# Two of six modulation tiles of a pair: scaled on ScalarE, added to the running sum by an accumulating transfer

## The chip, the cores and the metric

The kernel runs on one core of a Trainium2 chip. The metric is the device time of one execution in microseconds, and the number that counts is the median of the runs shown. The core has five engines that run side by side, each with an in-order queue of its own: TensorE (PE; its weight loads are listed apart as PEld), VectorE (DVE), ScalarE (ACT), GpSimd (POOL) and SyncE (SP, which here only issues transfers). Transfers run on 16 DMA engines, whoever issues them.

## The reference, cut to what matters

A two-layer trunk: layer 0 is RWKV-7 time mixing and a squared-ReLU MLP, layer 1 chunked band attention and a second MLP, with D = 2048 and 256 time steps. Every sub-layer is shifted, scaled and gated by a modulation vector that comes from one conditioning vector c:

```python
mod = c @ w_ada[layer] + b_ada[layer]              # (1, 2048) @ (2048, 12288)
sh1, sc1, gt1, sh2, sc2, gt2 = jnp.split(mod, 6, axis=-1)
h = modulate(rms_norm(x, g_mix[layer]), sh1, sc1)
y = rwkv7_time_mix(h, ...)                         # heads of 64; r, k, v, decay, a, g; a scan over time
x = x + gt1[:, None, :] * y
```

The modulation is a product of one vector with a large matrix, so almost all of its cost is in bringing the matrix in and passing over it once. Nothing of layer 0 after the time mixing, and nothing of layer 1, can start without its parts.

## The kernel before, in words

All matrix products run in split precision: a weight tile of 128x1024 is loaded (`raw`), ACT casts it to the high half `wH`, DVE subtracts to get the low half `wL` (`halves`, lines 413 to 424), and PE multiplies with both (`proj`, `proj2`).

The time mixing is the loop over slots of lines 1062 to 1100. The 2048 channels are 16 pairs of heads (128 channels each). A pair takes 8 slots of dense work on PE (its k and r products: `proj_steps`), and each pair also goes through 36 small steps, one to a slot: 8 early (decay, key norm, the scaled operands), 12 that invert a triangular matrix (`tt`, `u`, `iv`, with the masks `al` made by POOL), and 16 late (the recurrence over four chunks, group norm, gate). The small steps of several pairs share a slot, so each slot has: the small products of the live pairs, then two steps of dense products, then background work. From slot 128 on, the dense work is the output projection (`out_steps`).

The background work of a slot hangs on `(slot + lead) % S`, with S = 8, called the slot's remainder below. At 1, 3, 6 and 7 a weight tile is halved (`w_make`). At 0, 1, 2, 4, 6 and 7, from the second pair on, one modulation tile is stepped (`ada`, `ada_step`). The sum of a modulation half (1024 columns) is made in one buffer, `acc`, which is 128 rows of partial sums: 16 tiles of 128x1024, one for each row block `kt` of the matrix. Tile 0 sets the sum with one tensor_scalar (line 499), tiles 1 to 15 add to it with one scalar_tensor_tensor on DVE (line 501): `acc = raw * c[kt] + acc`. After tile 15, 32 small products on PE (`ada_sum`) add up the rows, and DVE adds the bias (line 527). `ADA_A` = 111 tiles are stepped in this stage; the rest follow in later stages.

A modulation tile is loaded by SP into a ring of three buffers (`rada`, `ada_room(3)`); `ada_fill` issues a load as soon as fewer than two tiles wait. SP also issues the weight loads, in one queue with these.

What sets the order: the program is traced in the order of the loop, and a planner then orders each engine's queue by its own estimates of when operands are there. `issue_after` and `behind` pin some work behind a named instruction of the same engine: the background work stands behind the last marked small step on ACT and on DVE. Nothing is marked on POOL or SP. Semaphores hold an instruction until its operands are there, and everything behind it on that engine waits with it.

POOL's work in this stage is small elementwise steps of the pairs: lines 180, 188, 190, 201, 205 of the early steps, 255, 256, 259 and 284 of the inversion. No transfer is issued by POOL anywhere in the kernel.

Of the kernel before, what the change touches and what calls it, by code (L numbers as in the profile page):

```python
# [14 lines left out]
AF = mybir.ActivationFunctionType  # L15
ALU = mybir.AluOpType
# [5 lines left out]
KT = D // P  # L22
# [347 lines left out]
class Body:  # L370
# [116 lines left out]
            self.ada_q.append((key, half, kt, raw))  # L487
        return tile_ is not None

    def ada_step(self):  # L490
        nc = self.nc
        if not (self.ada_q or self.ada_load()):
            return
        key, half, kt, raw = self.ada_q.popleft()
        ck = self.ct[:, kt:kt + 1]
        if kt == 0:
            self.fin(HK)
            self.acc = self.wp.tile([P, HK * P], F32, tag="acc", bufs=1, name="acc")
            nc.vector.tensor_scalar(out=self.acc, in0=raw, scalar1=ck, scalar2=0.0, op0=ALU.mult, op1=ALU.add)
        else:  # L500
            nc.vector.scalar_tensor_tensor(out=self.acc, in0=raw, scalar=ck, in1=self.acc, op0=ALU.mult, op1=ALU.add)  # L501
        if kt == KT - 1:
            self.fins = self.ada_sum(self.acc, self.mods[key], half, self.ada_src(*key)[1])
            if not self.lazy:
                self.fin(HK)
            if half == KT // HK - 1:
                self.ada_done.add(key)
# [23 lines left out]
        for _ in range(n):  # L531
            next(self.fins, None)

    def ada(self, n=1):
        for _ in range(n):
            self.ada_step()
        self.ada_fill()

    def mark(self, ins):
# [224 lines left out]
    def layer_a(self, st, sp):  # L764
        nc, tc, d = self.nc, self.tc, self.d
# [7 lines left out]
        with ExitStack() as s1:  # L773
# [9 lines left out]
            for q in range(4):  # L783
                (nc.sync if q % 2 else nc.scalar).dma_start(out=h[:, 4 * q:4 * q + 4, 1:T + 1],
                                                            in_=d["x"][:, 4 * q:4 * q + 4, :])
# [197 lines left out]
        with ExitStack() as s1:  # L983
# [16 lines left out]
            def proj_steps(pr):  # L1000
                for dst, hl in (("k", xk), ("r", xr)):
                    if dst == "r" and pr.j < 2:
                        ps = pp.tile([P, 2, T], F32, tag="lt", bufs=2, name="pj")[:, 0, :]
                    else:
                        ps = pp.tile([P, 2 * T], F32, tag="pj", bufs=1, name="pj")[:, :T]
                    for kt in range(KT):
                        if kt % HK == 0:
                            w = [self.w_made.popleft()] * (KT // HK)
                        self.proj(ps, w, lambda kt: hl[:, kt, :, 0:T], (kt, kt + 1))
                        if dst == "k" and kt == 1:  # L1010
                            if pr.j:
                                lw1 = pw.tile([P, 2, P], F32, tag="lw", bufs=1, name="lw")
                                nc.sync.dma_start(out=lw1, in_=d["lora2"][pr.j, :, 0:2])
                            pr.lw = lw1 if pr.j else lw0
                        if kt % 2 == 1:
                            if kt == KT - 1:
                                t = pw.tile([P, T], F32, tag=dst, bufs=2, name=dst)
                                nc.scalar.copy(t, ps)  # L1018
                                setattr(pr, dst, t)
                            yield  # L1020
# [36 lines left out]
            S, lead = self.SLOTS, self.LEAD  # L1057
# [4 lines left out]
            for slot in range(S * NPAIR + Pair.STEPS - lead):  # L1062
                live = []
                for j, pr in enumerate(pairs):
                    at = slot + lead - S * (j + 1)
                    if 0 <= at < Pair.STEPS:
                        if at == 0:
                            pr.gen = pr.steps()
                        sums = at in (Pair.STEPS - 3, Pair.STEPS - 1)
                        live.append((0 if at in inverts else 1 + (at < Pair.EARLY) + 2 * sums, -at, pr))  # L1070
                        pr.done = at == Pair.STEPS - 1
                self.small_steps([(o, -at, pr) for o, at, pr in sorted(live, key=lambda x: x[:2])])
                last = self.last_pe()
                if slot < S * NPAIR:
                    if slot % S == 0:
                        dense = proj_steps(pairs[slot // S])
                    todo = 16 // S
                else:
                    if outs is None:
                        self.y_hl = self.new_hl()  # L1080
                        outs = dense = out_steps()
                    n = int(sum(pace[:slot + 1 - S * NPAIR]))
                    todo, n_out = n - n_out, n
                with tc.issue_after(last):
                    for _ in range(todo):
                        next(dense, None)
                with tc.issue_after(self.last_pe()):
                    self.fin(HK)
                if outs is not None:
                    j = len(self.y_split)  # L1090
                    if j < KT - 1 and pairs[j].done:
                        self.split(self.y_hl, j, v[:, j, :])
                        self.y_split.append(j)
                if slot + lead == 2 * S - 4:
                    self.ada_fill()
                with self.behind():
                    if (slot + lead) % S in (1, 3, 6, 7):
                        self.w_make()
                    if slot + lead >= 2 * S and (slot + lead) % S in (0, 1, 2, 4, 6, 7):
                        self.ada()  # L1100
            for _ in dense:
                pass
            self.ada_drain(3)
# [123 lines left out]
    def attention(self, st, pp, scaled, kv_gain, kv_shift):  # L1227
# [8 lines left out]
        def projected(src, hl, dst, ada, between=()):  # L1236

            between = iter(between)
            w = self.weight(src)
            ps = pp.tile([P, 2, T], F32, tag="pj", bufs=2, name="pj")  # L1240
            for q in range(0, KT, 4):
                ins = self.proj2(ps, w, lambda kt: hl[:, kt, :, 0:T], (q, q + 4))
                with tc.issue_after(ins):
                    next(between, lambda: None)()
            self.sum2(dst, ps)
            self.ada(ada)
# [175 lines left out]
```

## Time and profile before

| | |
|---|---|
| median of 3 runs | 2601.4 us (2600.03 to 2603.03) |
| the profiled execution's own time | 2600.04 us |
| its span, first to last instruction | 2598.3 us |
| DVE accumulates of modulation tiles (line 501), whole kernel | 360, 462.7 us |
| the same that set the sum (line 499), whole kernel | 24 |
| loads of modulation tiles after the first stage | 384 of 512 KB |
| POOL's busy time, whole kernel | 229.2 us, 9% of the span |

How to read it: busy times are unions of an engine's instructions; a matmul's end is modelled, so PE's busy time has some slack in it. In a timeline row the first number is the start in us, the second the length, then engine, line, operation, `out<-in`, shapes and count; a bracket at the end gives how long the engine sat idle before and what released it. In a row of waits stand the total in us, the number of times and the longest. A name like SPq is an engine's queue of issues.

### The profile page before, as it was taken

The page shows a single profiled execution, that of the slowest core. Times are in us where ns is not written, and L with a number is a line of the kernel's source. Part 1 is how long each engine was busy: PE and PEld are TensorE (multiplying, and loading weights), DVE is VectorE, ACT ScalarE, POOL GpSimd, SP SyncE. Part 2 cuts the span into 40 slices and gives each one's busy share as a digit, 9 for nine tenths or more (in the row PEclk, how much of TensorE's full clock was granted, in tenths as well). Part 3 has the DMA queues.
Part 4 walks back from the last instruction along what each step waited for, and adds up shares of the span by engine and source line. Part 5 has one row for each costly group of instructions (what it writes and reads, how often), then busy time and mean ns, then how long its engine had stood idle before and what let it go on. Part 6 is the DMA issues. An engine that isn't in the chain of part 4 may idle for free.

```text
span 2598.3 us, 58875 instructions
## 1 busy us (share of the span) xinstructions
PE 2541.2 (98%) x24018; PEld 2225.7 (86%) x24018; DVE 2075.9 (80%) x3020; ACT 1371.4 (53%) x2535; POOL 229.2 (9%) x336
## 2 busy tenths in 40 slices
PE   6998999999999999999999999999999999999998
PEld 4788888888998888888888988887998888888887
DVE  6888889998899888888889898899896555556555
ACT  3346666674565364464455554565564463553554
POOL 0003333331200000000001000000100000000001
PEclk9999999999999999999999999999999999999999
DMA  9966666667869899888898688887676555555553
GB/s 364 366 232 195 216 213 223 212 217 222 307 220 338 322 329 343 326 323 316 313 323 291 201 305 304 309 277 261 233 258 212 187 187 188 187 188 191 187 187 130
DMA packets 207119, 662.65 MB, mean 255 GB/s; under 512 B 21248, under 2 KB 53632, under 8 KB 206848
## 3 DMA queue, kind: packets, MB, share of 16 engines
q1 hardware_dynamic: 205072, 657.02, 73.1%
q8 instruction: 188, 3.08, 0.5%
q10 hardware_dynamic: 1776, 1.87, 0.2%
q14 instruction: 83, 0.68, 0.1%
HBM read 656.71 MB, written 2.10 MB: 254 GB/s over the span
## 4 chain that ended last, share of the span: by engine, by line
PE 80%; DVE 10%; issue 4%; ACT 3%; DMA 2%; POOL 1%; SPq 0%; ACTq 0%; DVEq 0%; POOLq 0%
PE pj L454 43%; PE pj L456 21%; DVE acc L501 3%; PE pj L443 3%; PE pj L444 2%; PE pj L445 2%; DVE wL L423 2%; PE lt L588 1%; PE o L443 1%; DMA rada<-w_ada 1%; ACT wH L420 1%; PE o L444 1%; PE o L445 1%; ACT da L252 1%; PE pT L1310 0%
## 5 line engine op out<-in xcount | busy, mean ns | idle before, releaser
L423 DVE TENSOR_TENSOR wL<-raw,wH 128x1024 fp32r<-128x1024 f32 x771 | 946.6, 1229 | 336.7 <-ACT wH L420 334.1
L420 ACT CAST wH<-raw 128x1024 fp32r<-128x1024 f32 x771 | 805.3, 1045 | 729.6 <-PE pj L454 579.0
L454 PE MATMUL pj<-aHL,wH 128*128 128x512 f32 x2816 | 894.0, 398 | 1.2 <-DVE x L1135 1.1
L454 PE MATMUL pj<-hHL,wH 128*128 128x512 f32 x2048 | 644.2, 396 | 0.0
L456 PEld LDWEIGHTS pj<-aHL,wL 128*128 128x128 f32 x2816 | 531.7, 189 | 124.2 <-issue 0.3
L456 PE MATMUL pj<-aHL,wL 128*128 128x256 f32 x2816 | 563.0, 281 | 0.0
L501 DVE SCALAR_TENSOR_TENSOR acc<-rada,ct,acc 128x1024 f32<-128x1024 f32 x360 | 462.7, 1285 | 9.5 <-DMA rada<-w_ada 9.1
L456 PEld LDWEIGHTS pj<-hHL,wL 128*128 128x128 f32 x2048 | 384.2, 188 | 91.1 <-DVE wL L423 0.7
L454 PEld LDWEIGHTS pj<-aHL,wH 128*128 128x128 f32 x2816 | 431.6, 189 | 8.9 <-issue 8.5
L456 PE MATMUL pj<-hHL,wL 128*128 128x256 f32 x2048 | 402.0, 278 | 0.3 <-DVE wL L423 0.3
L454 PEld LDWEIGHTS pj<-hHL,wH 128*128 128x128 f32 x2048 | 312.0, 189 | 1.3 <-DVE hHL L1181 1.1
L443 PE MATMUL pj<-aHL,wH 128*128 128x256 f32 (+1 forms) x896 | 263.4, 294 | 1.5 <-ACT r L1018 1.4
L444 PE MATMUL pj<-aHL,wH 128*128 128x256 f32 (+1 forms) x896 | 253.7, 283 | 0.0
L445 PE MATMUL pj<-aHL,wL 128*128 128x256 f32 (+1 forms) x896 | 252.5, 282 | 0.0
L620 POOL TENSOR_TENSOR ss<-ss,sq 128x256 f32<-128x256 f32 x56 | 52.7, 942 | 1579.7 <-ACT sq L619 1532.1
L443 PEld LDWEIGHTS pj<-aHL,wH 128*128 128x128 f32 x896 | 169.8, 189 | 6.1 <-ACT r L1018 2.1
L1206 DVE SCALAR_TENSOR_TENSOR x<-pj,mod,x 128x256 f32<-128x256 f32 x256 | 123.4, 482 | 64.1 <-PE pj L456 61.1
L444 PEld LDWEIGHTS pj<-aHL,wH 128*128 128x128 f32 x896 | 169.6, 189 | 0.8
L445 PEld LDWEIGHTS pj<-aHL,wL 128*128 128x128 f32 x896 | 170.1, 190 | 0.2
L1178 ACT ACTIVATE t<-t 128x256 f32<-128x256 f32 x112 | 46.8, 418 | 119.6 <-DVE t L1150 119.6
L1181 DVE TENSOR_TENSOR hHL<-t,hHL 128x256 fp32r<-128x256 f32 x128 | 53.9, 421 | 1.8 <-ACT t L1180 1.1
L1180 ACT ACTIVATE t<-t 128x256 f32<-128x256 f32 x128 | 53.3, 416 | 3.3
(270 smaller groups left out, 2757.9 us busy)
## 6 DMA issues: line engine op xcount, KB each, us to landing
rada<-w_ada SPq DMA_DIRECT2D x320, 512.0 KB, 5.2
raw<-w_up SPq DMA_DIRECT2D x256, 512.0 KB, 4.1
raw<-w_down SPq DMA_DIRECT2D x256, 512.0 KB, 3.8
rada<-w_ada_kv SPq DMA_DIRECT2D x64, 512.0 KB, 6.3
rawa<-w_ada SPq DMA_DIRECT2D x32, 512.0 KB, 9.1
rawa<-w_ada_t SPq DMA_DIRECT2D x32, 512.0 KB, 8.6
raw<-w_k SPq DMA_DIRECT2D x32, 512.0 KB, 5.0
raw<-w_r SPq DMA_DIRECT2D x32, 512.0 KB, 4.0
```

The costliest lines, as they stand in the source:

```text
L420: nc.scalar.copy(Hf, raw)
L423: eng.tensor_tensor(out=Lf, in0=raw, in1=Hf, op=ALU.subtract)
L443: nc.tensor.matmul(ps, H[:, i, :], a(kt)[:, 0, :], start=(first and kt == 0), stop=False)
L444: nc.tensor.matmul(ps, H[:, i, :], a(kt)[:, 1, :], start=False, stop=False)
L445: ins = nc.tensor.matmul(ps, L[:, i, :], a(kt)[:, 0, :], start=False, stop=(last and kt == KT - 1))
L454: nc.tensor.matmul(ps, w[kt // HK][0][:, kt % HK, :], a(kt), start=(kt == 0), stop=False)
L456: ins = nc.tensor.matmul(ps[:, 0, :], w[kt // HK][1][:, kt % HK, :], a(kt)[:, 0, :], start=False, stop=(kt == KT - 1))
L501: nc.vector.scalar_tensor_tensor(out=self.acc, in0=raw, scalar=ck, in1=self.acc, op0=ALU.mult, op1=ALU.add)
L620: (eng or nc.gpsimd).tensor_tensor(out=self.ss, in0=self.ss, in1=sq, op=ALU.add)
L1180: nc.scalar.activation(t, t, AF.Square)
L1181: nc.vector.tensor_tensor(out=h[:, 1, :], in0=t, in1=h[:, 0, :], op=ALU.subtract)
L1206: nc.vector.scalar_tensor_tensor(out=x, in0=ps[:, i, :], scalar=self.mods[(layer, 5)][:, n:n + 1], in1=x, op0=ALU.mult, op1=ALU.add)
```

## The change

In the slots of remainder 2 and 4 the loop now calls `ada(moved=True)`. A tile that is stepped there, unless it is the first or the last of its sum, is multiplied by c[kt] on ACT in place, and POOL issues a transfer from the tile to `acc` that adds to what is there. The other tiles are stepped as before. An accumulate on DVE that follows a transfer waits for its landing, and so does a transfer that follows another; a tile's buffer can be loaded again once its transfer has landed.

```diff
-    def ada_step(self):
+    def ada_step(self, moved=False):
         ...
+        elif moved and kt < KT - 1:
+            nc.scalar.activation(raw, raw, AF.Copy, scale=ck)
+            nc.gpsimd.dma_start(out=self.acc, in_=raw, accum_op=ALU.add)
         else:
             nc.vector.scalar_tensor_tensor(out=self.acc, in0=raw, scalar=ck, in1=self.acc, op0=ALU.mult, op1=ALU.add)
...
-    def ada(self, n=1):
+    def ada(self, n=1, moved=False):
         for _ in range(n):
-            self.ada_step()
+            self.ada_step(moved)
         self.ada_fill()
...
                     if slot + lead >= 2 * S and (slot + lead) % S in (0, 1, 2, 4, 6, 7):
-                        self.ada()
+                        self.ada(moved=(slot + lead) % S in (2, 4))
```

## The prediction

> **What bounds the kernel now.** I read the page first. PE is busy nearly throughout, but that is a share over stages with different limits, so it says little about this one.
>
> ```profile
> span 2598.3 us, 58875 instructions
> ...
> PE 2541.2 (98%) x24018; PEld 2225.7 (86%) x24018; DVE 2075.9 (80%) x3020; ACT 1371.4 (53%) x2535; POOL 229.2 (9%) x336
> ...
> q1 hardware_dynamic: 205072, 657.02, 73.1%
> ```
>
> The change acts only in time mixing. The windows below (columns: length; busy us and instructions of PE, PEld, DVE, ACT, POOL; granted clock; DMA share; GB/s) cut it out, from the first tile that can be moved to the point where the output projection fills the stage.
>
> ```profile
> 226.00:293.00 67.00, 62.80 (x1502) 56.43 (x1497) 61.51 (x104) 39.81 (x108) 24.98 (x29) 1.00 0.71 226
> 293.00:420.00 127.00, 123.77 (x2971) 111.94 (x2971) 114.89 (x205) 83.23 (x245) 47.13 (x60) 1.00 0.67 215
> 420.00:549.00 129.00, 125.44 (x3039) 113.50 (x3039) 117.60 (x212) 83.76 (x246) 48.96 (x60) 1.00 0.68 221
> 549.00:640.00 91.00, 86.00 (x2008) 76.15 (x2008) 79.53 (x142) 53.40 (x162) 25.12 (x35) 0.98 0.67 210
> sum 414.00, PE 398.00 PEld 358.02 DVE 373.53 ACT 260.20 POOL 146.19; mean PE 99.50 PEld 89.51 DVE 93.38 ACT 65.05 POOL 36.55
> ```
>
> In these 414.0 us PE is idle for 414.0 - 398.0 = 16.0 us, DVE for 40.5. In the two steady windows PE idles 3.2 and 3.6 us, under 3%. So two engines are nearly full, and whatever is taken from DVE, at most 16.0 us can come out unless PE's own work shrinks, which the change doesn't touch. The granted clock is 1.00 (0.98 in the last window), so no throttle hides in it.
>
> The chain of waits tells it from the other side. For 293 to 549 us it gives most to DVE:
>
> ```profile
> by line: DVE acc L501 15.8%; DVE wL L423 13.0%; issue 6.2%; ACT wH L420 3.7%; ACT da L252 3.2%; PE pj L443 3.0%; PE lt L588 2.9%; PE pj L445 2.6%; PE pj L444 2.6%; PE iv L135 2.4%; DVE s L174 2.2%; DVE s L195 2.1%; DVE sq L149 2.0%; DVE kr
> ```
> ```profile
> L501 DVE SCALAR_TENSOR_TENSOR acc<-rada,ct,acc 128x1024 f32<-128x1024 f32 x57 | 72.7, 1276 | 0.0
> ```
>
> The 57 accumulates in that window have 15.8% of 256 us, 40.4 us, on the chain. Both readings are true: the chain follows the last releaser, and PE is released by DVE again and again, but only just. One pair in the timeline shows how much "just" is. DVE's rows around it:
>
> ```profile
> 400.67 1.30 DVE L501 SCALAR_TENSOR_TENSOR acc<-rada,ct,acc 128x1024 f32<-128x1024 f32 x1
> ...
> 402.92 1.25 DVE L501 SCALAR_TENSOR_TENSOR acc<-rada,ct,acc 128x1024 f32<-128x1024 f32 x1
> ...
> 407.96 0.42 DVE L196 SCALAR_TENSOR_TENSOR s<-s,k 128x256 f32<-128x256 f32 x1
> ...
> 409.51 1.27 DVE L501 SCALAR_TENSOR_TENSOR acc<-rada,ct,acc 128x1024 f32<-128x1024 f32 x1
> ...
> 411.59 0.30 DVE L266 STREAM_TRANSPOSE tt<-u 128x128 f32<-128x128 f32 x1
> ...
> 414.21 1.28 DVE L501 SCALAR_TENSOR_TENSOR acc<-rada,ct,acc 128x1024 f32<-128x1024 f32 x1
> 415.40 1.22 DVE L423 TENSOR_TENSOR wL<-raw,wH 128x1024 fp32r<-128x1024 f32 x1
> ...
> 417.08 1.24 DVE L501 SCALAR_TENSOR_TENSOR acc<-rada,ct,acc 128x1024 f32<-128x1024 f32 x1
> ...
> 420.38 0.42 DVE L246 TENSOR_TENSOR ar<-gr,csts 128x256 f32<-128x256 f32 x1
> ...
> 422.63 0.75 DVE L499 TENSOR_SCALAR acc<-rada,ct 128x1024 f32<-128x1024 f32 x1
> ```
> ```profile
> 411.45 0.28 PE L445 MATMUL pj<-aHL,wL 128*128 128x256 f32 x1
> 412.03 0.35 PE L135 MATMUL iv<-tt,al 32*32 32x32 f32 x20 [0.31 <-DVE tt L266]
> ```
>
> The accumulates at 402.92 and 409.51 are the two to be moved (slot remainders 2 and 4); 400.67, 414.21 and 417.08 are the neighbours that stay (1, 6, 7). Behind 409.51 comes the transpose at 411.59, and PE waits 0.31 us for it. That is what two accumulates of 1.2 us each, standing on the chain, cost PE in this pair. The table of waits for 226 to 640 us sums it:
>
> ```profile
> PE iv L135 <- DVE tt L266: 3.4, 7, 1.2
> ```
> ```profile
> PEld iv L135 <- POOL al L259: 2.4, 5, 0.9
> PEld pj L443 <- ACT r L1018: 2.1, 5, 0.6
> ```
>
> **The change part by part.** *How many.* 111 tiles are stepped in this loop, six to a pair in the order of remainders 0, 1, 2, 4, 6, 7. Tile i is moved if i mod 6 is 2 or 3 and its row block i mod 16 is neither 0 nor 15: 37 candidates, less i = 32 and 80 (block 0), less 15 and 63 (block 15): 33, two to a pair, in 17 pairs.
>
> *Removed from DVE.* 33 accumulates:
>
> ```profile
> L501 DVE SCALAR_TENSOR_TENSOR acc<-rada,ct,acc x104: 1242/1275/1864, 226.5 to 663.3; 128x1024 f32<-128x1024 f32 x104
> ```
>
> 33 x 1.275 = 42.1 us of DVE work. DVE has it off the path wherever PE is the later one. What comes back is PE's waiting that ends behind these accumulates: for the transpose 3.4 us in 7 waits, and for ACT's copy of r, which stands behind the accumulate of remainder 2, 2.1 us on the loading side in 5. Together 5.5 us, none longer than 1.2 us, which is what one accumulate holds DVE (402.92 to 404.1). Those are the limits: 0 to 5.5; I take 4.0, since behind a released PE the next wait (a copy, al, issue) is near.
>
> *Added to ACT.* 33 scalings of 128x1024 in place. The trace has no such activation; the nearest rows:
>
> ```profile
> L167 ACT ACTIVATE s<-s,csts 128x512 f32<-128x512 f32 x10 | 7.2, 725 | 0.3
> ```
> ```profile
> 403.03 0.42 ACT L176 ACTIVATE e<-s 128x256 f32<-128x256 f32 x1 [1.01 <-DVE s L174]
> ...
> 409.90 0.21 ACT L324 COPY g<-lt 128x64 f32<-128x64 f32 x1 [2.60 <-PE lt L588]
> ...
> 413.80 1.05 ACT L420 CAST wH<-raw 128x1024 fp32r<-128x1024 f32 x1
> ```
>
> The cast of such a tile (413.80) is 1.05 us; from 128x512 (0.73), twice that, 1.45, bounds it above. I take 1.05, by the same shape. Both places have cover: ACT is idle 1.01 us before 403.03 and 2.60 us before 409.90, and the raw tiles are loaded ahead. Cost 0; the larger price would stick out of the first gap by 0.44 us, 17 x 0.44 = 7 us, the upper bound. Without cover, r's copy behind it on ACT, for which PE waits, would be late by the whole 1.05 in 17 pairs: 18 us.
>
> *Added to POOL.* 33 DMA issues. No DMA of POOL is in the trace. SP's issue is 0.33 us, the longest ordinary POOL row here 1.65; I take 1.0, the middle, since the lower end is another engine's.
>
> ```profile
> 404.90 0.64 POOL L188 TENSOR_SCALAR s<-s,vecs 128x256 f32<-128x256 f32 x1
> 408.46 0.84 POOL L205 TENSOR_TENSOR kh<-s 128x256 f32<-128x256 f32 x1 [2.92 <-DVE s L196]
> 409.73 1.65 POOL L201 TENSOR_TENSOR bh<-bh,s 128x256 f32<-128x256 f32 x1 [0.43 <-DVE s L195]
> 422.31 0.41 POOL L255 TENSOR_TENSOR u<-da,csts 128x128 f32<-128x128 f32 x1 [10.93 <-ACT da L252]
> ```
>
> The first issue, at about 403.1, stands before L188 (ends 405.54), whose product DVE reads at 407.96, or 1.2 us earlier once the accumulate is gone: slack 1.2 us, so 1.0 is covered and 1.65 would cost 0.45 a pair, 8 us in all. The second finds POOL idle between 409.30 and 409.73 or from 411.38 to 422.31. Waiting for the first transfer's landing, it can hold back only L201 (bh), and that only if it is queued ahead of it; L255, on the path to al, stands 11 us later. Cost 0.
>
> *Added to the DMA engines.* 33 transfers of 512 KB within SBUF that read source and destination. Durations of the loads of that size:
>
> ```profile
> L410 SPq DMA_DIRECT2D rada<-w_ada x100: 327/328/677, 227.8 to 638.8; - x100
> ...
> DMA to landing us min/median/max: 3.0/4.5/6.7
> ```
> ```profile
> DMA to landing us min/median/max: 3.3/5.4/11.0
> ```
>
> A load lands after 4.5 us in this stage (3.0 to 6.7; 11.0 at worst in the kernel). By the page's queue row, 657.02 MB took 73.1% of 2598.3 us, so 0.524 MB takes 1.5 us of all sixteen engines; a second stream to read adds about that. Bounds 3.0 and 11.0; I take 4.5 + 1.5 = 6.0 us from issue to landing. With DMA share 0.67 the 33 x 3 = 99 us of engine time over 414 fits.
>
> *The new wait.* The next accumulate on DVE (remainder 6, 414.21) reads the sum that the second transfer writes, and the second transfer must wait for the first. First issue 403.1, landing 409.1; second issue 409.3 to 411.4, landing 415.3 to 417.4. So the accumulate at 414.21 comes 1 to 3 us later; behind it on DVE stand the subtraction at 415.40, the add and transpose for PE, the accumulate at 417.08 and L246 at 420.38. If the queue has the subtraction ahead of the accumulate, DVE idles only until ACT's cast ends (413.80 + 1.05 = 414.85), 0.6 us instead of 1 to 3. This delays L246, from which ACT, then POOL (u, al), then PE go on; PE waits for al already in 5 places (2.4 us). I put 0.6 us on the 5 pairs without slack: +3.0, less 1.0 for pairs where L246's other operands are late anyway: +2.0. Bounds 0 and 1.6 us in all 17 pairs, 27.
>
> *SP.* A moved tile's buffer is free at landing, not at the end of the accumulate: the load behind it goes 5 to 7 us later. Of remainder 4's buffer that is the load for the tile at 422.63: 417.4 + 4.5 = 421.9, in time by 0.7. By the code four weight tiles are loaded ahead of use. Cost 0, up to what the third rival says.
>
> *Sum:* -4.0 + 0 + 0 + 2.0 + 0 = -2.0 us.
>
> A rule beside this: "DMA: Bandwidth & Descriptors" of the Trainium skill (Anatomy of one DMA) gives a transfer from GpSimd's queue about 2.0 us plus bytes over 436 GB/s, an estimate of 3.2 us for 512 KB. By it the second landing would be before 414.21, the new wait nothing, and the sum -4.0; the trace's loads of that size, from the other queue, take 4.5.
>
> **The rivals.**
>
> *DVE was the bound (faster).* The chain gives accumulates 40.4 us for 57; for 33 that is 23.4, capped by PE's 16.0 us of idle. For it: DVE's backlog carries over, so waits for al or "issue" may also shrink. Against: the steady windows hold 6.8 us of idle PE in all. Price -12 to -16; -14 gives 2587.
>
> Beside it: "Trainium Kernel Development and Optimization" of the Trainium skill (Performance Expectations) calls matmul busy time a bad metric and LDWEIGHTS busy share a good one. That share is 225.4 of 256 us here, 88%; by it PE would have 12% of room, and this rival would hold.
>
> *The landing takes the place of the accumulate (slower).* Place: DVE's accumulate of remainder 6. If the transfer takes 6.7 + 1.5 = 8.2 us, the landings are 411.3 and 419.6; the accumulates of 414.21 and 417.08 both move in front of L246, and DVE loses about 1.6 us that it can't fill. Decides from about 7 us a transfer, where the second landing passes 418.3 and the row at 417.08 is late too. For it: DMA share 0.67, and a queue in fixed order. Against: pairs have slack before al is used. Price from 6 pairs x 1.6 - 4.0 = +6 to 17 x 1.6 - 4.0 = +23; +14 gives 2615.
>
> *The sum's own chain becomes the bound.* Per pair: two transfers, then a load of 4.5 into the buffer freed by the second, two accumulates and the scaling's hand-over, some 8 us.
>
> ```profile
> L162 DVE TENSOR_SCALAR s<-ms x10: 683/684/689, 293.3 to 523.7; 128x512 f32<-128x512 f32 x10
> ```
> ```profile
> 663.31 1.28 DVE L501 SCALAR_TENSOR_TENSOR acc<-rada,ct,acc 128x1024 f32<-128x1024 f32 x1
> ...
> 688.39 1.76 DVE L501 SCALAR_TENSOR_TENSOR acc<-rada,ct,acc 128x1024 f32<-128x1024 f32 x1
> ```
>
> A pair takes (523.7 - 293.3) / 9 = 25.6 us, so it decides from (25.6 - 8) / 2 = 8.8 us a transfer. At 11.0 it slips 4.4 us a pair, 75 in 17 pairs, of which the 25 us between the last accumulate of the stage and the next one are free: +50, 2651. Against: no load in this stage takes over 6.7.
>
> **How the numbers follow.** The profiled execution took 2600.04 us (its span is 2598.3); the runs' median is 2601.4, 1.4 above. 2600.04 - 2.0 + 1.4 = 2599.4. Chances: this forecast 0.42 (own range 2595 to 2606, from -5.5 with the new wait at nothing to +5), faster rival 0.21, landing 0.26, chain 0.11. The range reaches to the faster rival's price and past the middle of the landing's: 2586 to 2621; outside lie the chain and the landing's worst.
>
> About 0.2%, 5.2 us, is what can be told from no change. Faster: 0.20 of the faster rival and 0.08 of the forecast, 0.28. Slower: 0.23 of landing, 0.11 and 0.03 of the forecast, 0.37. Same: 0.35.
>
> **What would show it.** Right: DVE's busy time in 226 to 640 us falls by some 40 us, ACT's rises by some 32, PE's idle stays between 10 and 20; transfers land within 7 us. The relief is wrong if PE's idle falls under 6. The new wait is wrong if DVE's accumulates behind a transfer never wait, or wait over 1 us in most pairs. POOL's term is wrong if L188 ends after DVE wants it. The forecast falls if transfers take 9 us or more, or if the issue holds POOL far over 1.65 us.

## The result and the profile after

The changed kernel takes 2681.35 us (2677.96 to 2686.41, four runs) against 2600.99 us (2600.03 to 2603.03): a ratio of 1.0301 [1.0288, 1.0314], 80 us slower. The prediction was 2599.4 us, with a range up to 2621.

The page of the profiled execution (2678.34 us), its first lines and the row of the new queue:

```profile
span 2676.6 us, 59006 instructions
...
PE 2567.6 (96%) x24018; PEld 2248.5 (84%) x24018; DVE 2040.4 (76%) x2987; ACT 1410.9 (53%) x2568; POOL 236.3 (9%) x369
...
q0 software_dynamic: 4752, 17.30, 3.4%
```

DVE has 35.5 us less to do and ACT 39.5 us more: the work moved as planned. But PE, with the same 24018 products, is busy 26 us longer and idle besides. Where, the windows of the prediction show again (length; busy us and instructions of PE, PEld, DVE, ACT, POOL; granted clock; DMA share; GB/s):

```profile
226.00:293.00 67.00, 53.89 (x1162) 47.85 (x1164) 47.00 (x78) 39.24 (x95) 25.62 (x35) 0.92 0.74 218
293.00:420.00 127.00, 117.23 (x2760) 106.10 (x2759) 94.96 (x175) 83.30 (x223) 39.62 (x56) 0.95 0.74 223
420.00:549.00 129.00, 114.06 (x2659) 103.00 (x2657) 93.63 (x178) 83.75 (x225) 44.45 (x63) 0.95 0.74 223
549.00:640.00 91.00, 82.25 (x1880) 74.42 (x1878) 69.62 (x132) 61.81 (x170) 32.05 (x46) 0.94 0.74 216
sum 414.00, PE 367.44 PEld 331.37 DVE 305.21 ACT 268.09 POOL 141.74; mean PE 91.86 PEld 82.84 DVE 76.30 ACT 67.02 POOL 35.43
```

PE's idle time in these 414 us went from 16.0 to 46.6, and the granted clock from 1.00 (0.98 in the last window) to between 0.92 and 0.95. DVE isn't full any more (305 of 414 us): it waits.

The same clock time isn't the same work, so the fair cut is one of the program: from the first L162 to the first update of x in the output projection. Before, then after:

```profile
203.50:670.70 467.20, 446.92 (x9999) 403.70 (x9998) 412.89 (x713) 287.57 (x816) 151.58 (x192) 0.99 0.68 219
```
```profile
204.60:751.30 546.70, 478.62 (x10037) 431.60 (x10036) 378.91 (x680) 328.96 (x850) 160.12 (x225) 0.93 0.74 220
```

This stretch is 79.5 us longer, and that is the whole loss. Two parts make it. PE's idle time is length less busy: 20.3 before, 68.1 after, +47.8. The time that the clock takes is (1 - granted clock) x length: 0.01 x 467.2 = 4.7 before, 0.07 x 546.7 = 38.3 after, +33.6. What is left of PE's work is 442.2 and 440.3 us, the same within the rounding of the clock (0.005 x 500 = 2.5 us). The same two parts are given for every run below; there the rest of PE's work lies between 437.0 and 451.3 us, so up to 9 us of a run's stretch stand in neither part.

The clock's part follows from the idle part. A stretch of after around one idle time of PE (same columns):

```profile
300.40:302.30 1.90, 0.06 (x4) 0.06 (x6) 1.34 (x2) 0.55 (x2) 0.00 (x0) 1.00 0.91 323
302.30:303.10 0.80, 0.80 (x21) 0.73 (x22) 0.00 (x0) 0.50 (x2) 0.00 (x0) 0.98 1.00 384
303.10:306.50 3.40, 3.40 (x50) 3.11 (x52) 3.14 (x4) 1.71 (x5) 0.00 (x0) 0.50 0.71 237
306.50:310.00 3.50, 3.50 (x68) 3.19 (x72) 1.49 (x4) 3.34 (x12) 0.04 (x1) 1.00 0.83 279
```

PE stands still for 1.9 us; 0.8 us later the clock is halved for 3.4 us, which costs another 1.7. In the stretch after there are 14 such halvings, 78 us long together; before there are 2, 6.8 us. The Trainium skill ("TensorE: Matmul & The Clock Gate", What's actually happening) gives half rate after an idle window of about 3.4 us; the trace agrees on the halving and on its unit of 3.4 us, but shows it behind idle times of 1.3 to 2.8 us too.

What PE waits for, from the table of waits of 203 to 760 us (the row of SP, whose queue issues the loads, from 203 to 640 us):

```profile
DVE acc L504 <- DMA acc<-rada: 69.5, 18, 9.3
...
PE iv L135 <- DVE tt L266: 30.0, 15, 6.0
...
DVE s L196 <- POOL s L188: 12.7, 12, 1.6
```
```profile
SPq L410 <- DMA acc<-rada: 139.7, 24, 8.3
```

Three of the prediction's small terms are large here. DVE's accumulate (now L504) waits 69.5 us for landings, 18 times; PE waits 30 us for the transpose, where it was 3.4. L196 waits for L188 in 12 pairs (12.7 us; 1.0 in 2 before). And SP's queue stands at the reload of a moved tile's buffer until the transfer lands; before, its loads stood for accumulates, 83.4 us in 36 places. One pair on DVE:

```profile
411.15 0.28 DVE L341 TENSOR_SCALAR zs<-lt,pc 128x64 f32<-128x64 f32 x1 [0.85 <-ACT sa L330]
414.75 1.28 DVE L504 SCALAR_TENSOR_TENSOR acc<-rada,ct,acc 128x1024 f32<-128x1024 f32 x1 [3.32 <-DMA acc<-rada]
415.95 1.22 DVE L423 TENSOR_TENSOR wL<-raw,wH 128x1024 fp32r<-128x1024 f32 x1
417.09 0.28 DVE L289 TENSOR_TENSOR u<-u,iv 128x128 f32<-128x128 f32 x1
417.40 0.31 DVE L266 STREAM_TRANSPOSE tt<-u 128x128 f32<-128x128 f32 x1
```

The planner put the accumulate of remainder 6 ahead of the subtraction, the add and the transpose. It waits 3.32 us, and they wait with it.

### The profile page after: what moved, and what is told of

Its sections match the earlier page's. It is cut to its first block, busy times and chain, and to the rows that moved or that the text cites. A ratio compares the mean times of both kernels' runs of the same rounds, so it can differ in the third digit from the quotient of the medians.

```text
span 2676.6 us, 59006 instructions
## 1 busy us (share of the span) xinstructions
PE 2567.6 (96%) x24018; PEld 2248.5 (84%) x24018; DVE 2040.4 (76%) x2987; ACT 1410.9 (53%) x2568; POOL 236.3 (9%) x369
## 4 chain that ended last, share of the span: by engine, by line
PE 69%; DMA 2%; DVE 2%; issue 1%; ACT 0%; DVEq 0%; ACTq 0%; SPq 0%; POOLq 0%
PE pj L454 41%; PE pj L456 20%; PE pj L444 2%; PE pj L443 2%; PE pj L445 2%; DMA acc<-rada 1%; DMA rada<-w_ada 1%; DVE wL L423 1%; DVE acc L504 1%; PE pT L1313 0%; PE m L526 0%; PE po L1320 0%; PE S L1292 0%; PE S L1291 0%; DMA raw<-w_q 0%
## 5 line engine op out<-in xcount | busy, mean ns | idle before, releaser
L504 DVE SCALAR_TENSOR_TENSOR acc<-rada,ct,acc 128x1024 f32<-128x1024 f32 x327 | 420.0, 1285 | 80.1 <-DMA acc<-rada 69.5
L443 PE MATMUL pj<-aHL,wH 128*128 128x256 f32 (+1 forms) x896 | 267.6, 299 | 0.2
L444 PE MATMUL pj<-aHL,wH 128*128 128x256 f32 (+1 forms) x896 | 256.6, 286 | 1.5 <-issue 1.5
L1181 ACT ACTIVATE t<-t 128x256 f32<-128x256 f32 x112 | 46.9, 419 | 120.0 <-DVE t L1153 120.0
L135 PE MATMUL iv<-tt,al 32*32 32x32 f32 x1920 | 29.9, 199 | 32.5 <-DVE tt L266 30.0
L135 PEld LDWEIGHTS iv<-tt,al 32*32 32x32 f32 x1920 | 23.5, 111 | 39.8 <-issue 31.1
```

The source lines that it names most:

```text
L135: self.b.nc.tensor.matmul(o[QS[K], c, :], lhsT[QS[R], c, :], rhs[QS[R], c, :], start=True, stop=True, tile_position=(H * R, H * K))
L443: nc.tensor.matmul(ps, H[:, i, :], a(kt)[:, 0, :], start=(first and kt == 0), stop=False)
L444: nc.tensor.matmul(ps, H[:, i, :], a(kt)[:, 1, :], start=False, stop=False)
L1181: nc.scalar.activation(t, t, AF.Relu)
```

## The experiments

All times are medians; "before" is the kernel before on the same chip (2604 to 2608 us; 2601 for the change itself), and a difference in us is (ratio - 1) x that median. First the table to look things up in. Idle and clock are the two parts worked out above, over the same stretch of each run's program, from the one execution that was profiled. The DMA share is that of the added transfers' queue between 203 and 670 us. The last column adds up the idle times of PE over 0.8 us that end 1.0 to 1.7 us behind the end of a code fetch, between 220 and 600 us (explained under "What of a transfer costs").

| run | ratio [95%] | us against before | PE idle | clock | added DMA share | behind a fetch |
|---|---|---|---|---|---|---|
| before | 1 | 0 | 20.3 | 4.7 | 0 | 0.8 |
| VectorE adds | 0.9993 [0.9981, 1.0004] | -2 | 21.4 | 9.4 | 0 | 4.0 |
| left out | 0.9964 [0.9952, 0.9976] | -9 | 17.6 | 4.6 | 0 | 2.9 |
| held | 1.0008 [0.9998, 1.0018] | +2 | 23.7 | 14.3 | 0 | 7.0 |
| 4 KB onto itself | 1.0011 [0.9997, 1.0026] | +3 | 23.6 | 9.5 | 1.6% | 6.0 |
| 512 KB plain, ScalarE's queue | 1.0043 [1.0027, 1.0059] | +11 | 35.0 | 9.8 | 8.7% | 19.6 |
| 512 KB plain, GpSimd's queue | 1.0091 [1.0067, 1.0115] | +24 | 41.0 | 15.0 | 8.4% | 19.1 |
| 256 KB onto itself | 1.0086 [1.0063, 1.0109] | +22 | 39.4 | 20.0 | 9.6% | 18.9 |
| 512 KB onto itself | 1.0190 [1.0155, 1.0226] | +50 | 56.8 | 15.7 | 17.3% | 20.5 |
| the same, issued later | 1.0110 [1.0093, 1.0127] | +29 | 39.6 | 15.1 | 18.0% | 10.7 |
| the same, fewer loads | 1.0096 [1.0076, 1.0115] | +25 | 40.8 | 14.9 | 18.4% | 13.8 |
| own buffer, 256 KB | 1.0122 [1.0099, 1.0145] | +32 | 39.6 | 20.0 | 9.4% | 14.2 |
| unread load, 256 KB | 1.0047 [1.0032, 1.0062] | +12 | 33.5 | 9.8 | 6.2% | 7.2 |
| unread load, 4 KB | 1.0038 [1.0025, 1.0052] | +10 | 28.3 | 9.6 | 0.4% | 4.6 |
| half tile | 1.0163 [1.0131, 1.0195] | +43 | 49.5 | 20.6 | 8.9% | 13.2 |
| half tile, staged | 1.0118 [1.0098, 1.0137] | +31 | 41.2 | 25.3 | 9.4% | 11.6 |
| later step | 1.0201 [1.0176, 1.0227] | +52 | 56.1 | 26.4 | 16.7% | 23.5 |
| both orders | 1.0175 [1.0156, 1.0193] | +46 | 50.5 | 20.7 | 17.2% | 4.6 |
| after | 1.0301 [1.0288, 1.0314] | +78 | 68.1 | 38.3 | 15.9% | 8.9 |

### Is it the accumulate's wait?

**VectorE adds.** Only the scaling moves.

```diff
-            nc.gpsimd.dma_start(out=self.acc, in_=raw, accum_op=ALU.add)
+            nc.vector.tensor_tensor(out=self.acc, in0=raw, in1=self.acc, op=ALU.add)
```

> The tile is scaled on ScalarE in place as in the change, but added by VectorE (a tensor_tensor in the place of the transfer); no transfer, no issue on GpSimd. Theory W (the accumulate of remainder 6 waits for the landing on VectorE, and the small steps that TensorE needs wait behind it): without a landing the kernel is back at 2595 to 2610 us, slightly over before if the hand-over from ScalarE costs something. Rival A (ScalarE's 33 x 1.16 us delay r's copy): 2620 us or more, since ScalarE does the same. Rivals P (GpSimd's issue ahead of line 188) and C (the transfers' load on the DMA engines) also forecast about 2601.

Measured 2603.42 us, 0.9993 [0.9981, 1.0004]. ScalarE's 33 scalings (1.16 us each) cost nothing.

**512 KB onto itself.** Scaling, issue and bytes stay; nothing reads what the transfer writes.

```diff
-            nc.gpsimd.dma_start(out=self.acc, in_=raw, accum_op=ALU.add)
+            nc.gpsimd.dma_start(out=raw, in_=raw, accum_op=ALU.add)
```

> Scaling, issue and accumulating transfer as in the change, but the transfer adds the tile to itself, so nobody waits for its landing but the reload of its buffer; the moved tiles are left out of the sum. Theory W: the 80 us go away, 2590 to 2605 us, below before if the relief of VectorE is worth anything. Rival P: the issue still stands ahead of line 188, which VectorE waited for 12 times for 12.7 us in all: 2608 to 2615. Rival C: traffic is the same, so 2660 or more.

Measured 2653.76 us, in none of the three ranges. So the theory that the wait is the whole loss falls: 50 us are lost where no accumulate waits for the sum, and PE waits 2.4 us for the transpose in place of 30.0 (203 to 670 us). What the wait adds is the rest, 1.0301 - 1.0190, some 29 us.

**Later step.** The tile of remainder 6 is stepped in the slot of remainder 7.

```diff
-                    ... (slot + lead) % S in (0, 1, 2, 4, 6, 7):
-                        self.ada(moved=(slot + lead) % S in (2, 4))
+                    ... (slot + lead) % S in (0, 1, 2, 4, 7):
+                        self.ada(1 + ((slot + lead) % S == 7), moved=(slot + lead) % S in (2, 4))
```

> As the change, but the tile of remainder 6 is stepped in the slot of remainder 7 (two there), so that the accumulate behind a transfer comes one slot, some 3 us, later. Theory W: a landing takes 6.5 us, the wait in the trace is 3.3 us in most pairs: most of the 80 us go, 2605 to 2630 us. Rivals P and C: no change, 2670 or more.

Measured 2657.87 us, between the theories. With a slot between, DVE waits 30.8 us for landings in 13 places in place of 69.5 in 18 (203 to 760 us), and PE's wait for the transpose is gone (203 to 670 us):

```profile
PE iv L135 <- DVE tt L266: 2.3, 5, 0.9
```

26 us come back: the same third of the loss from the other side.

**Half tile.** Columns 0 to 511 by ScalarE and transfer, the rest on VectorE.

```diff
+            h = HK * P // 2
+            nc.scalar.activation(raw[:, :h], raw[:, :h], AF.Copy, scale=ck)
+            nc.gpsimd.dma_start(out=self.acc[:, :h], in_=raw[:, :h], accum_op=ALU.add)
+            nc.vector.scalar_tensor_tensor(out=self.acc[:, h:], in0=raw[:, h:], scalar=ck, in1=self.acc[:, h:], ...)
```

> As the change, but only the first 512 of a moved tile's 1024 columns go by ScalarE and the transfer; VectorE adds the other 512. Theory W: the landing of 256 KB is about 1.5 us shorter (half of the streams' time), two such landings stand ahead of the wait but only the second shows: the wait falls from 3.3 to about 2 us a pair, 2640 to 2660 us. If landing is mostly a fixed time: 2670 or more. Rival A: half of ScalarE's time gone, 2640.

Measured 2647.17 us, in theory W's range, with 39.1 us of DVE's waits for landings in 13. It halves the bytes as well as the wait, so it doesn't part the two.

### Issue, ring, or traffic?

Four runs take the tile-onto-itself run apart. The floor first: **left out** deletes the transfer line.

> The two moved tiles of a pair are scaled by ScalarE in place and then left out of the sum: no transfer, no issue on GpSimd, no addition on VectorE. It is the floor under the run with the transfer onto itself (2653.8 us). Theory P (the issue on GpSimd stands ahead of the small-step work that L196 needs), theory R (the ring of three tiles is held until the landing, so loads come late) and theory C (the traffic itself) all say 2590 to 2605 us, since each of their causes is gone. Theory O (the planner's other order of the engines, or the missing work on VectorE, costs by itself) says above 2625 us.

Measured 2597.65 us. Without the 33 accumulates, and with nothing in their place, the kernel is 9 us faster [0.9952, 0.9976]. That is what there was to gain.

**4 KB onto itself** (`out=raw[:, 0:8], in_=raw[:, 0:8]`):

> As the run with the transfer onto itself, but the transfer moves only columns 0 to 7 of the scaled tile onto themselves (4 KB in place of 512 KB); the moved tiles are left out of the sum. Issue, its place in GpSimd's queue and its wait for ScalarE stay; the bytes go. Theory P: 2640 to 2660 us, L196 again waiting for L188 some 15 us in sum. Theory C (traffic): 2590 to 2610. Theory R (ring held): in between, as far as the landing stays long; with a landing of 2 us in place of 7, 2605 to 2625 and the accumulates' waits for reloads well under the 24.3 us.

Measured 2610.55 us. L196 waits for L188 14.0 us in 12 again, of which 8.0 in 12 stand in the run without any issue too ("left out"), since VectorE's queue has L196 earlier there than before; and SP's queue stands 132.0 us in 28 at the landing (median 3.9 us from the issue), yet the kernel is as fast as before. Issue, its place and a short hold cost 12 us over the floor, not 59: theory P falls as the main cause.

**512 KB plain on ScalarE's queue** (`nc.scalar.dma_start(out=raw, in_=raw)`):

> As the run with the transfer onto itself, but a plain transfer of the scaled tile onto itself, issued on ScalarE's queue behind the scaling: nothing is added to GpSimd; the moved tiles are left out of the sum. The bytes and the hold of the ring stay. Theory P: 2595 to 2612 us and no wait of L196 for L188 above 2 us in sum, unless ScalarE's issue is as long as GpSimd's and delays ScalarE's own small steps. Theories R and C: 2640 to 2660, with VectorE's accumulates waiting for reloads some 24 us in sum as before.

Measured 2618.78 us, between the two theories. The transfers land in 5.5 us, not 6.9, and use half the engine time; the twins below take that up.

**Issued later:** the issue is kept for one slot and pinned behind GpSimd's last two instructions.

```diff
+            last = [i for i in self.nc.cur_bb.bb.instructions if i.engine == pool][-2:]
+            with self.tc.issue_after(last[0]), self.tc.issue_after(last[1]):
+                self.nc.gpsimd.dma_start(out=raw, in_=raw, accum_op=ALU.add)
```

> As the run with the transfer onto itself, but the issue is put off by one slot and fixed behind the last two GpSimd instructions emitted by then (so behind L190 and L188 for the tile of remainder 2, behind L201 and L205 for that of remainder 4); the moved tiles are left out of the sum. Theory P: 2600 to 2620 us and the wait of L196 for L188 back to 1 to 3 us in sum. Theories R and C: 2650 to 2675 (the ring is held one slot longer, so the waits for reloads grow above 24 us).

Measured 2635.29 us, between the two ranges: 21 us of the 50 come back, more than the issue with 4 KB cost in all. The place matters, but more so where the transfers are heavy.

Then the hold of the ring. **Held:** no transfer; two slots after the scaling ScalarE copies 8 columns of the tile onto themselves.

> No transfer and no GpSimd issue: the moved tiles are scaled by ScalarE and left out of the sum, and two slots later (about 6.4 us) ScalarE copies columns 0 to 7 of the tile onto themselves, which holds the ring's tile about as long as a landing. Theory R: 2630 to 2660 us, with SyncE's reloads waiting over 100 us in sum for that copy. Theory C: 2595 to 2608, as without the transfer (2597.7).

Measured 2607.90 us. SP waits 82.0 us in 17 for that copy (up to 8.4), and the cost is 11 us over the floor. SP waits 150.5 us in 26 in the run with 512 KB onto itself, so this hold is the lighter one; but with 4 KB SP waited 132.0 us, at 12 us over the floor. Theory R falls as the main cause.

**Own buffer and 256 KB onto itself**, meant as twins with and without the hold:

```diff
+            nc.scalar.activation(self.own, raw[:, :HK * P // 2], AF.Copy, scale=ck)
+            nc.gpsimd.dma_start(out=self.own, in_=self.own, accum_op=ALU.add)
```

> ScalarE writes the scaled first 512 columns of a moved tile into a buffer of its own, and GpSimd's transfer adds that buffer (256 KB) onto itself; the moved tiles are left out of the sum. The tile of the ring is free when ScalarE has read it, so no load waits for a landing. Theory R (the loss without a waiting accumulate comes from the ring: SyncE's queue stands at the reload until the landing, 150.5 us in 26 in the run with the whole tile onto itself): 2598 to 2612 us, near the run with a 4 KB transfer (2610.6), and SyncE's waits for a landing gone. Theory C (the bytes of the transfers slow the loads): half the bytes, so about half of what the whole tile costs over the 4 KB one (43 us): 2625 to 2640.

> The twin of the run with the buffer of its own: the first 512 columns of a moved tile are scaled in place and transferred (256 KB) onto themselves in the ring's tile; the moved tiles are left out of the sum. Same bytes, same issue, but the ring's tile is held until the landing. Theory R: above the twin by what the hold costs: 2620 to 2645 us, with SyncE's waits for the landing above 100 us in sum and VectorE's accumulates waiting for reloads. Theory C: equal to the twin within 5 us.

Measured 2635.61 and 2627.35 us. The first says nothing: with one buffer, ScalarE stood 42.8 us in 12 places at the landing of the transfer before, a wait that the changed kernel doesn't have. The second, with half the bytes, loses about half of what the whole tile does.

**Half tile, staged**, the whole sum with the ring freed early and the later step:

> The whole sum, with both suspected causes of the loss taken out for half of each moved tile: ScalarE writes the scaled first 512 columns into a buffer of its own, GpSimd's transfer adds that buffer to the sum's first half, VectorE adds the other half itself, and the tile of remainder 6 is stepped in the slot of remainder 7. The ring's tile isn't held by the landing, and one slot lies between the landing and the next accumulate. If the hold of the ring and the accumulate's wait are the whole loss: 2600 to 2618 us (the 4 KB transfer showed 2610.6 with what is left). If the bytes matter too: 2620 to 2640.

Measured 2637.42 us. It has the same single buffer as the own-buffer run, and ScalarE stood 48.6 us in 13 places at it; it only shows that this version doesn't save the change.

### What of a transfer costs

In the traces of all runs with large transfers, PE stands still for 1 to 4 us at times where nothing that the profile shows has just ended. One in the run with 512 KB onto itself, PE's rows, and the DMA queues between 522.9 and 525.6 us:

```profile
522.65 0.33 PE L591 MATMUL lt<-ar,sa 64*64 64x64 f32 x2
525.51 0.27 PE L591 MATMUL lt<-ar,sa 64*64 64x64 f32 x2 [2.54 <-issue]
```
```profile
q1 hardware_dynamic: 201, 0.74, 85.0%
q8 instruction: 1, 0.02, 2.3%
```

Four products of one kind, and PE stops in the middle of them; "issue" says that no wait is known. In that time the DMA engines are 85% busy with loads, and one fetch of code (q8) runs, from 523.15 to 524.12 us. PE goes on 1.4 us after its end. The long unexplained idle times end so, 1.1 to 1.6 us behind a fetch; the last column of the table adds up all idle times that do. A fetch comes every 6.0 us or so (78 between 203 and 670 us before), so by chance some 12% of idle times would fall in a span of 0.7 us; of the 16 idle times over 0.8 us in the plain run 11 do.

The traces hold a sharper test. A run has 188 such fetches of 16 KB, and PE's queue has 188 times 256 records (matmuls, weight loads and those of its sequencer). Counted from the start, each of the 275 idle times of PE of 0.1 us or more that read "issue", in this stretch of all 19 kernels, ends at the same place of the count, 193 or 194 records beyond a multiple of 256. And taking the fetches and these places in order, one each, PE passes none sooner than 1.06 us behind the end of its fetch, in 1501 cases. So PE stands there because the next 256 instructions aren't in yet. This part of its idle time is 6.1 us before, 11.4 with 4 KB onto itself, 24.0 with the plain 512 KB, 27.8 with the adding ones, and 15.3 in the changed kernel. A fetch itself takes no longer (median 0.97 us in the plain run, 0.98 before); some of them start later: one in ten starts more than 4.2 us behind the place before it in the plain run, 3.2 before. Why they start later isn't shown; no run changed the fetches alone.

**Unread load**, 256 KB and 4 KB: the kernel before, with two loads a pair into a buffer that nobody reads, on GpSimd's queue; the same order on every engine in both.

```diff
+            self.nc.gpsimd.dma_start(out=self.own, in_=self.d["w_ada"][0][0:P, 0:n_])
```

> The kernel before, with two more loads a pair: GpSimd's queue loads 256 KB of HBM into a buffer that nobody reads (some 33 in the time mixing, fixed in GpSimd's order behind the two instructions emitted last). Nothing is moved, nothing waits for the buffer but its next load. Theory F (the added bytes keep the fetches of TensorE's code late; TensorE then stands still, and its clock is halved after that): 2612 to 2632 us, and idle times of TensorE over 0.8 us that end 1.0 to 1.7 us behind the landing of a code fetch add up to 7 to 20 us between 220 and 600 us, where before has 0.8. Theory E (it is the edges of the moved work, and bytes alone cost nothing): within 0.3% of before, 2599 to 2613.

> The twin with 4 KB in place of 256 KB in each added load: the same instructions in the same order on every engine, without the bytes. Both theories: 2600 to 2613 us, and the idle times behind code fetches at 0.8 to 6 us. If it is as slow as its twin, GpSimd's issue is the cause and not the bytes.

Measured 2617.21 and 2614.08 us. The first number is in the range of theory F, but its twin, just above its own range, is as slow within the intervals: 256 KB more of loads cost about 3 us, which these runs can't tell from nothing, and the issues 10. Without the twin this would have passed for a proof.

**Fewer loads:** the moved tiles aren't loaded, and the tile that VectorE used last is transferred in their place.

> The run with the whole tile onto itself, but the moved tiles aren't loaded at all: ScalarE scales and the 512 KB transfer adds onto itself the tile that VectorE has used last, so the transfers' bytes stand in the place of the loads' bytes; the moved tiles are left out of the sum. Theory F: 2597 to 2618 us in place of 2653.8, with idle times behind code fetches under 8 us (20.5 there). If such transfers cost by themselves, whatever else the queues carry: 2630 to 2655.

Measured 2628.87 us, between the two. The loads' share fell from 57.2% to 49.2% while the adding transfers kept theirs, and 25 of the 50 us came back; all queues together are as busy as before (49.2 + 18.4 against 66.6%). So a fuller DMA isn't the whole of it either. Here one tile is held over both transfers, and ScalarE stands 24.9 us in 12 places (203 to 670 us) at the landing of the first before it scales the tile again, a wait that the run with 512 KB onto itself doesn't have. So a new cost may stand in this run beside the saving, and the two weren't parted.

**512 KB plain on GpSimd's queue**, an exact twin of 512 KB onto itself: the same instructions in the same order, only without `accum_op`.

> The twin of the run with the whole tile onto itself (2653.8 us): the same instructions in the same order on every engine, and the same 512 KB on GpSimd's queue, but the transfer is plain and doesn't add; the moved tiles are left out of the sum. Theory D (what costs is the time that the transfers hold the DMA engines: the adding ones took 17.3% of the sixteen engines between 203 and 670 us for 14.68 MB, plain ones on ScalarE's queue 8.7% for 15.85 MB): with half the time, about half of the 43 us over the 4 KB transfer: 2622 to 2640 us. Theory B (the bytes count, however they are moved): 2645 to 2660.

Measured 2630.17 us, in the range of theory D: 26 us less than its adding twin. The queue's rows between 203 and 670 us, adding first:

```profile
q1 hardware_dynamic: 27936, 89.67, 57.2%
q0 software_dynamic: 4032, 14.68, 17.3%
```
```profile
q1 hardware_dynamic: 28823, 92.26, 60.0%
q0 software_dynamic: 4320, 15.73, 8.4%
```

The adding transfer takes 17.3% x 467 us / 28 = 2.9 us of all sixteen engines, the plain one 8.4% x 467 / 30 = 1.3 us; per megabyte 1.18% against 0.53%. Landing went from 6.9 to 5.3 us. This is the one run that parts a cause cleanly: the addition, not the 512 KB, is half of what the transfer onto itself costs.

PE's idle time tells the two halves apart, one profiled execution each. From 4 KB to the plain 512 KB it grows by 17.4 us, 12.6 of them at late code. From plain to adding it grows by 15.8, only 3.8 at late code; the rest ends at named waits, for POOL's `al` above all (10.1 us in 8 against 3.3 in 4), while DVE's accumulates wait longer for reloads that come late. DVE's row from 203 to 760 us, adding first:

```profile
DVE acc L504 <- DMA rada<-w_ada: 38.4, 17, 5.6
```
```profile
DVE acc L504 <- DMA rada<-w_ada: 17.0, 11, 4.6
```

**Both orders:** the change itself, with the issue later and the later step.

> The whole sum, and both orders mended: GpSimd issues the transfer of the changed kernel one slot later behind the two instructions emitted last, and the tile of remainder 6 is stepped in the slot of remainder 7. If the two orders add up (the later step alone 2657.9 us; the later issue took 18 us off the run with the tile onto itself): 2635 to 2655 us, slower than before still. If the orders are the whole loss: 2600 to 2615.

Measured 2649.62 us: 32 us better than the change as it is, 46 us worse than before. DVE's waits for landings are 33.7 us in 14, no fewer than with the later step alone, and the transfers start later. The queues' order doesn't save the change, and nothing tried here that computes the whole sum beats the kernel before by more than it can be measured.

## Why the prediction was wrong

The loss from the floor up, each line a difference of two runs of the table in us against before:

| | us |
|---|---|
| 33 accumulates gone, scaling on ScalarE ("left out") | -9 |
| issue on GpSimd, short hold of the ring ("4 KB onto itself") | +12 |
| 512 KB copied ("512 KB plain, GpSimd's queue") | +21 |
| the copy adds ("512 KB onto itself") | +26 |
| an accumulate waits for it (after) | +29 |
| sum | +78, rounded |

This is one path through the runs, and not a list of what PE waits for in the changed kernel. There 33.1 of PE's 68.1 us of idle time end at the transpose, and 15.3 at late code, less than the 27.8 in the run with 512 KB onto itself.

*What held.* The counts, the scaling's cover (0 us; 1.16 us each, 1.05 taken), the issue's length (0.85 to 1.03 us, 1.0 taken) and the landing (median 6.5 us, 6.0 taken; 5.1 to 8.5). Even the engines' time was right: 1.5 us for the stream that is read and as much again for the sum's, 3.0 us, where 2.9 were measured with 512 KB onto itself.

```profile
L501 ACT ACTIVATE rada<-rada,ct x33: 1135/1157/1177, 227.2 to 738.9; 128x1024 f32<-128x1024 f32 x33
L502 POOL DMA_DIRECT2D acc<-rada x33: 852/892/1027, 229.3 to 740.5; - x33
```

The Trainium skill's estimate of 3.2 us for this transfer ("DMA: Bandwidth & Descriptors", Anatomy of one DMA) is half of the landing measured. The same page (Rules for kernel authors) says that an adding transfer reads its destination and writes it later; the doubled engine time of the twins agrees.

*The relief*, -4.0 with limits 0 to 5.5, was mis-sized: the floor is -9 [-12.5, -6.3]. The limits came from named waits. Where the other 5 us lie isn't shown: the profile of "left out" has PE idle 17.6 us against 20.3, only 2.7 less. The faster rival put -14 there, within PE's 16 us of idle time; the floor is about halfway between it and the forecast. It is far from the 12% of room that the rule on LDWEIGHTS of the Trainium skill ("Trainium Kernel Development and Optimization", Performance Expectations) would have left.

*The DMA engines' term* failed first: "With DMA share 0.67 the 33 x 3 = 99 us of engine time over 414 fits." An average that fits was taken as a cost of nothing. Copy and addition cost 21 + 26 us. The 2.9 us of all sixteen engines fall within one landing of 6.9, among loads that land late with it: the median landing of the loads of w_k in 203 to 670 us went from 5.2 before to 6.5 with the plain 512 KB and 7.1 with the adding ones (but only 5.3 in the changed kernel), and code came late.

*The new wait*, +2.0 with bounds 0 to 27, failed by its size: "0.6 us on the 5 pairs without slack". That stood on the subtraction running ahead of the accumulate. The queue has it behind, with the add and the transpose, and so it had before: the prediction's own rows show the accumulate at 414.21 and the subtraction at 415.40. The wait is 3.32 us in the pair shown and 69.5 in 18, and it costs 29 us. The path was wrong too. The delay was to reach PE over L246 and `al`, but PE's wait for `al` hardly changed (2.3 us in 3 before, 2.6 in 4 after); it came over the transpose that stands right behind, 3.4 before, 30.0 after. The rival of the landing had the place right, and the sign "wait over 1 us in most pairs" is what came, but it too went over L246, let the wait decide only from 7 us a transfer and put the whole change at +23 at most. The wait alone cost 29 at 6.5 us.

*POOL's term*, 0: L188 was to have 1.2 us of slack. L196 waits for it 12.7 us in 12, so the slack wasn't there; but 8.0 in 12 of that come without any issue, from L196 standing earlier in DVE's queue. With 4 KB transfers the same waits came and the kernel was as fast as before; with 512 KB the later issue took 21 us off.

*SP's term*, 0: the load behind a moved tile was to be in time by 0.7 us. SP's queue stands 139.7 us in 24 at that reload, and what is queued behind it waits too. A hold alone, of 82.0 us in 17, costs 11 us over the floor ("held").

*The clock* was ruled out: "no throttle hides in it". That was nearly true of before (two halvings in the stretch), and false of what makes PE idle for 1.3 us or more at a time. It is 33.6 of the 79.5 us of the stretch.

Each of these terms was bounded by itself, as if the others were nothing. Issue, hold and a load's bytes cost 10, 11 and 3 us each alone; issue, hold, copy and addition together make 59 over the floor. The copy's 21 us go with late code, and the addition's 26 with late reloads and late `al`; how many us each of these is worth, and how POOL's order acts on them, stays open, as no run changed one alone.

## What to carry to other kernels

Where two engines are both over 90% busy, work taken off one of them can be worth little: here 9 us for 42 of work; measure that floor by leaving the work out before building the version that moves it. An accumulating transfer within SBUF isn't free work: price its bytes twice, its landing as a wait for whatever stands behind the next use in an in-order queue, and its source buffer as held until the landing. Where PE is the bound, an idle time of more than about 1.3 us can cost a half-rate stretch of 3.4 us or more behind it as well: 14 of 18 such times had one begin within 3.5 us of their end in the changed kernel's stretch, 7 of 16 with 512 KB onto itself. And where PE stops with no cause named, count its records: here the stops at one place of every 256 were late code.

## What was not expected of the hardware

- The granted clock halves for 3.4 us or a multiple (up to 10.2 us) behind single idle times of PE from 1.2 us on (1.21 in the trace before), though not behind each: the one of 2.54 us shown above had none. In the changed kernel this costs 33.6 us beside 47.8 us of added idle time.
- An adding transfer within SBUF holds the DMA engines 2.2 times as long per byte as a plain one (1.18% against 0.53% of the engines per megabyte), and an adding one of 4 KB still lands only after 3.9 us; of 512 KB, a plain one lands after 5.3 and an adding one after 6.9.
- Every idle time of PE that reads "issue" (275 of 275 in the stretches) ends where its next 256 instructions (16 KB) begin, the long ones 1.1 to 1.6 us behind the end of their fetch. With 512 KB transfers these waits for code make 24.0 and 27.8 us, against 6.1 before. Why the fetches start late isn't shown.
